# Two blocks on one Trainium2 core: the second block's modulation summed by VectorE, ScalarE and GpSimd instead of TensorE

## The chip, the cores and the metric

The kernel runs on one core of one Trainium2 chip, as one program. The metric is the device time of one execution in microseconds (us), smaller is better. Before the change it was 3041.41 us, the median of three runs (3035.09, 3041.41 and 3043.16).

In the profile PE is TensorE (PEld its weight loads), DVE is VectorE, ACT is ScalarE, POOL is GpSimd and SP is SyncE, which issues nearly all DMAs. L280 is line 280 of the kernel.

## The reference

Two transformer blocks follow each other. The first works on 256 tokens of width 1024, in two layers; the second on the same 256 tokens and 256 context tokens, again in two layers, with a mixer of three branches and 32 experts. The second block is steered by a modulation that depends on two condition vectors alone (the sample's `c` and the context's `c_ctx`), not on the tokens:

```python
def first_block(...):
    h = x
    for i in range(DEPTH):                                  # 2
        g = norm_g[i]
        y = mixer_i(rms_norm(h, g[0]))                      # MLA, then dilated attention
        h = h + rms_norm(y, g[1])
        h = h + rms_norm(swiglu(rms_norm(h, g[2]), ffn_w_in[i], ffn_w_out[i]), g[3])
        h = h + (p[i] @ ple_w_proj[i]) * jax.nn.sigmoid(h @ ple_w_gate[i])
    return h

def ada_modulation(cond, w, b):
    m = cond @ w + b                                        # [1, 1024] @ [1024, 6144]
    return jnp.split(m[:, None, :], 6, axis=-1)

def second_block(x, c, ctx, c_ctx, w_ada, b_ada, ...):
    cond_lat, cond_ctx = jax.nn.silu(c), jax.nn.silu(c_ctx)[None]
    for l in range(DEPTH):                                  # 2
        sh1, sc1, gt1, sh2, sc2, gt2 = ada_modulation(cond_lat, w_ada[l], b_ada[l])
        csh1, csc1, cgt1, csh2, csc2, cgt2 = ada_modulation(cond_ctx, w_ada[l], b_ada[l])
        ...
```

## The kernel before, in words

The program goes through the first block phase by phase: `mla_layer`, `ffn_layer(0)`, `ple_layer(0)`, `dil_layer`, `ffn_layer(1)`, `ple_layer(1)`; then `second()` does the two layers of the second block. All matrix products with weights are float32 products made of three float32r products. A weight tile of 1 MB is loaded from DRAM into one of four `raw` buffers (`load_raw`, NRAW = 4); class `W` splits each half of it into `hi` (ScalarE cast, L279) and `lo` (VectorE subtraction, L280; in the first pair of tiles of a phase it is GpSimd's), each in one of three buffers (NSPLIT = 3); `mm3` issues the three matmuls (L291 to L293).

In `ffn_layer` one pass of the loop (a chunk) computes 256 of 2816 hidden features: two weight tiles, four halves, 96 matmuls of 256 columns; then, per 128 features, silu on ScalarE (L811), a product with the other half in PSUM on VectorE (L812), and the split of the result into `hidh` (ScalarE, L817) and `hidl` (VectorE, L818). There are 11 chunks in each of the two layers. In `dil_layer` each of four quads of heads takes nine such weight tiles of 48 matmuls each, and then its attention.

The modulation is background work: class `Ada` holds a generator per layer of the second block, and `fill(n)` emits n units of it at places of the first block that the table FILL gives. There are 48 units. A unit before loads 1 MB of `w_ada` (128 rows, 2048 columns) into a raw buffer and issues four matmuls (L888), one to each 32 rows of a PSUM bank; eight units accumulate one bank, which is then added to the bias rows `msb` (L892). After three banks, `msb` is transposed (L897), copied to `mod` (L898) and written to DRAM (`dm`, L899). Ten units lie in the attention of `mla_layer`, and by FILL 5 at its end, 10 in quads 2 and 3 of `dil_layer` and 8 at its end, 3 and 3 at the ends of the ffn layers, 3 and 5 at the ends of `ple_layer`; one is left to the start of `second()`.

Instructions stand on each engine in the order in which the tile framework places them, each engine executes its own in that order, and a buffer is given out anew when its readers are done.

Of the kernel before, what the change touches and what calls it, by code (L numbers as in the profile page):

```python
# [7 lines left out]
F32 = mybir.dt.float32  # L8
# [8 lines left out]
D = 1024  # L17
# [21 lines left out]
def build_consts():  # L39
# [36 lines left out]
    # relative bias of the dilated mixer: bucket one-hot over m = t - s + 127  # L76
# [7 lines left out]
    for g, dil in enumerate((1, 4, 16)):  # L84
# [16 lines left out]
def build(nc, tc, I, O, stop=""):  # L101
    """I: dict of input APs, O: output AP [256, 1024]."""
# [47 lines left out]
    def pipelined(n, stages, between=None):  # L150
        """stages[j](i) for items i < n, stage j of an item j steps after its first."""
# [11 lines left out]
    def blk(shape, dt=F32, name="blk", glob=False):  # L163
        """A block of the phase, or one that outlives it."""
# [84 lines left out]
    def load_exp(ap):  # L249
        """4 (or 2) k chunks of an expert's weight, also in buffers of split weights; k -> [128, width]."""  # L250
# [14 lines left out]
    class W:  # L265
        """Rows chunks of a weight tile as pairs (hi, lo)."""
# [29 lines left out]
    def rsqrt(ssq, n, inv_d):  # L296
        """(ssq * inv_d + eps) ** -0.5 for [128, n] sums of squares."""
# [570 lines left out]
    class Ada:  # L868
# [13 lines left out]
        def units(self):  # L882
            for c in range(3):
                p = ps_mm()
                for k in range(8):
# [4 lines left out]
                    if k < 7:  # L890
                        yield
# [869 lines left out]
```

## Time and profile before

| | |
|---|---|
| runs, median | 3041.41 us (3035.09 to 3043.16) |
| the profiled execution, span from its first to its last instruction | 3046.4 us |
| PE busy | 2842.3 us, 93% |
| DVE busy | 1383.3 us, 45% |
| ACT busy | 946.0 us, 31% |
| POOL busy | 384.1 us, 13% |
| HBM read | 697.91 MB, 230 GB/s over the span |
| mean granted TensorE clock | 0.971 |

The page gives no time of the profiled execution beside its span. The first block and the modulation fill about the first 1000 us, the second block the rest. The shares are means over stages with different limits: the busy shares of the stages that the change touches are read from windows of the trace.

### The profile page before, as it was taken

The numbers are of one execution on the slowest core, as the hardware profiler recorded it, in microseconds if no ns is written. First come the engines' busy times: TensorE is split into PE (matmuls) and PEld (weight loads), VectorE is DVE, ScalarE is ACT, GpSimd is POOL, SyncE is SP. The second block draws the span as 40 slices with busy tenths as digits, with TensorE's granted clock in tenths as the row PEclk, the third lists the DMA queues.
The fourth block names the chain that finished last, engine by engine and source line by source line (L and its number), as shares of the span: only waits on it lengthen the run. The fifth ranks groups of instructions, "written<-read, shape, count | busy, mean of one in ns | idle before, by whom it ended". The sixth has DMA issues, their size and how long they took to land. (4 is left out here: it accounts for less than half of the span.)

```text
span 3046.4 us, 39455 instructions
## 1 busy us (share of the span) xinstructions
PE 2842.3 (93%) x15583; PEld 1972.6 (65%) x15583; DVE 1383.3 (45%) x2942; ACT 946.0 (31%) x1630; POOL 384.1 (13%) x304
## 2 busy tenths in 40 slices
PE   7999999998999999999979999999799997999996
PEld 6699789886997786678764444443486894333332
DVE  6555555445555426533472333333537564222222
ACT  5444444333444333433331001010334442111111
POOL 1010000000000201101031322223201001111111
PEclk9999999999999999999989999999899998999999
DMA  6665665665656432113468889889432386999997
GB/s 201 232 204 189 213 207 155 193 201 180 197 184 221 154 93 47 59 49 97 141 228 327 347 347 359 331 346 395 143 125 69 123 278 253 409 398 409 409 409 300
DMA packets 317148, 702.36 MB, mean 231 GB/s; under 512 B 36055, under 2 KB 179694, under 8 KB 310686
## 3 DMA queue, kind: packets, MB, share of 16 engines
q1 hardware_dynamic: 316622, 698.20, 64.0%
q8 instruction: 125, 2.05, 0.3%
q10 hardware_dynamic: 336, 1.59, 0.1%
q14 instruction: 65, 0.53, 0.0%
HBM read 697.91 MB, written 1.81 MB: 230 GB/s over the span
## 5 line engine op out<-in xcount | busy, mean ns | idle before, releaser
L280 DVE TENSOR_TENSOR lo<-raw,hi 128x1024 fp32r<-128x1024 f32 (+1 forms) x404 | 500.7, 1240 | 573.3 <-ACT hi L279 572.4
L279 ACT CAST hi<-raw 128x1024 fp32r<-128x1024 f32 (+1 forms) x418 | 433.7, 1039 | 623.4 <-PE mm L292 341.9
L291 PE MATMUL mm<-xh,hi 128*128 128x256 f32 (+1 forms) x1728 | 544.2, 316 | 3.7 <-ACT hi L279 2.5
L292 PE MATMUL mm<-xl,hi 128*128 128x256 f32 (+1 forms) x1728 | 538.3, 312 | 0.5 <-DVE xl L944 0.5
L293 PE MATMUL mm<-xh,lo 128*128 128x256 f32 (+1 forms) x1728 | 535.2, 310 | 1.2 <-POOL lo L280 1.2
L291 PEld LDWEIGHTS mm<-xh,hi 128*128 128x128 f32 x1728 | 333.4, 193 | 45.1 <-issue 20.3
L1532 PE MATMUL mm<-raw,xq 128*64 128x512 f32 x1152 | 345.3, 608 | 7.1 <-DMA raw<-in_moe_w_up_dram 3.9
L293 PEld LDWEIGHTS mm<-xh,lo 128*128 128x128 f32 x1728 | 333.0, 193 | 18.4 <-issue 1.8
L292 PEld LDWEIGHTS mm<-xl,hi 128*128 128x128 f32 x1728 | 333.5, 193 | 17.5 <-issue 2.0
L1546 POOL TENSOR_TENSOR h<-h,res 128x512 f32<-128x512 f32 x120 | 150.2, 1273 | 758.0 <-DVE res L1544 713.5
L1544 DVE TENSOR_TENSOR res<-tp,gt 128x512 f32<-128x512 f32 x192 | 123.0, 684 | 235.7 <-PE tp L1542 235.7
L1532 PEld LDWEIGHTS mm<-raw,xq 128*64 128x64 f32 x1152 | 100.0, 139 | 175.5 <-issue 156.6
L1601 DVE SCALAR_TENSOR_TENSOR y<-mm,wsum,y 128x512 fp32r<-128x512 f32 x64 | 47.1, 749 | 306.0 <-ACT y L1600 304.0
L291 PE MATMUL mm<-hi,xh 128*128 128x512 f32 (+2 forms) x504 | 174.9, 349 | 0.0
L293 PE MATMUL mm<-hi,xl 128*128 128x512 f32 (+2 forms) x504 | 174.9, 347 | 0.0
L292 PE MATMUL mm<-lo,xh 128*128 128x512 f32 (+2 forms) x504 | 174.4, 346 | 0.0
L1532 PE MATMUL mm<-raw,hT 128*64 128x512 f32 x568 | 160.1, 597 | 12.8 <-ACT hT L1589 12.6
L1532 PE MATMUL mm<-hi,xq 128*64 128x512 f32 x428 | 167.4, 603 | 0.6 <-DMA hi<-in_moe_w_up_dram 0.6
L1532 PE MATMUL mm<-lo,xq 128*64 128x512 f32 x428 | 159.7, 593 | 0.0
L1505 ACT COPY xq<-tp 128x512 f32<-128x512 f32 x64 | 37.5, 587 | 348.6 <-PE tp L1503 348.6
L280 POOL TENSOR_TENSOR lo<-raw,hi 128x1024 fp32r<-128x1024 f32 x14 | 33.7, 2422 | 861.2 <-ACT hi L279 766.0
L1542 PEld LDWEIGHTS tp<-y,oht 128*128 128x128 f32 x384 | 63.7, 188 | 119.3 <-issue 47.9
(486 smaller groups left out, 4588.3 us busy)
## 6 DMA issues: line engine op xcount, KB each, us to landing
raw<-in_moe_w_gate_dram SPq DMA_DIRECT2D x77, 1024.0 KB
raw<-in_moe_w_down_dram SPq DMA_DIRECT2D x71, 1024.0 KB
raw<-in_moe_w_up_dram SPq DMA_DIRECT2D x67, 1024.0 KB
raw<-in_w_in_dram SPq DMA_DIRECT2D x56, 1024.0 KB
raw<-in_w_ada_dram SPq DMA_DIRECT2D x48, 1024.0 KB
raw<-in_ffn_w_in_dram SPq DMA_DIRECT2D x44, 1024.0 KB
raw<-in_dil_w_qkv_dram SPq DMA_DIRECT2D x36, 1024.0 KB
hi<-in_moe_w_up_dram SPq DMA_DIRECT2D x59, 512.0 KB
```

What stands on the lines that cost most here:

```text
L279: A.copy(hv, rv[:, k0:k0 + n, :])
L280: (eng or V).tensor_tensor(lv, rv[:, k0:k0 + n, :], hv.bitcast(F32), op=ALU.subtract)
L291: T.matmul(ps, lhsT=lh, rhs=rh, start=first, stop=False)
L292: T.matmul(ps, lhsT=lh, rhs=rl, start=False, stop=False)
L293: T.matmul(ps, lhsT=ll, rhs=rh, start=False, stop=last)
L1505: A.copy(xq[:, 2 * kk:2 * kk + 2, :], p.rearrange("p (a b) -> p a b", b=256))
L1532: T.matmul(p[n][64 * i:64 * i + 64, :], lhsT=lhs(k, i), rhs=rv[i][kk][:, n * 512:(n + 1) * 512], start=k == 0, stop=k == kn - 1)
L1542: T.matmul(p, lhsT=oht[:, t * 128:(t + 1) * 128], rhs=y[:, i, ns], start=i == 0, stop=i == 1)
L1544: V.tensor_tensor(tmp, p, gts[:, t // 2, ns], op=ALU.mult)
L1546: (G if P < 15 else V).tensor_tensor(hs, hs, tmp, op=ALU.add)
L1601: V.scalar_tensor_tensor(y[:, 1, ns], py[n], wsum, y[:, 0, ns].bitcast(F32), op0=ALU.mult, op1=ALU.subtract)
```

## The change

A unit now loads 1 MB of `w_ada` as two chunks of 128 rows for the 1024 columns of one of the six parameters. VectorE multiplies a row chunk by the sample's condition (one number per partition) and adds it to an SBUF sum (`acc[:, 0]`, one instruction of 1024 columns per row chunk). For the context's condition ScalarE multiplies into a buffer `mtmp` of 512 columns, of which there is one, and GpSimd adds that to `acc[:, 1]`, twice per row chunk. The first row chunk of a parameter writes the sums instead. After four units, four matmuls with a selecting matrix `sel` add up the partitions into a PSUM bank, which is added to `msb`. Four times six units per layer are 48 units, as before, and the same bytes. The units move: none in or after `mla_layer`, one in each chunk of both ffn layers, 22 in `dil_layer`, and 4 at ends of phases. For the memory, a pool `ada` is opened after `mla_layer`, and the temporary tables of the rope move to a small tile. The layout of `msb`, `mod` and `dm` is another.

```diff
-FILL = dict(mla_end=5, ffn=([0] * 11, [0] * 11), ffn_end=(3, 3), ple_end=(3, 5), dil_end=8,
-            dil=([0] * 9, [0] * 9, [1] * 5 + [0] * 4, [1] * 5 + [0] * 4))
+FILL = dict(mla=0, mla_end=0, ffn=([1] * 11, [1] * 11), ffn_end=(1, 1), ple_end=(1, 0), dil_end=1,
+            dil=([1, 0, 1, 0, 1, 0, 1, 0, 1], [1, 0, 1, 0, 1, 0, 1, 0, 1], [1, 0, 1, 1, 0, 1, 1, 0, 1],
+                 [1, 0, 1, 1, 0, 1, 1, 0, 1]))
...
-        condT = cpool.tile([128, 8, 36], F32, name="condT")
-        V.memset(condT, 0.0)
+        condT = cpool.tile([128, 8, 2], F32, name="condT")
+        sel = cpool.tile([128, 40], F32, name="sel")
+        V.memset(sel, 0.0)
+        V.memset(sel[:, 8:9], 1.0)
...
-            for c in range(3):
+            condT = late["condT"]
+            for i in range(6):
+                acc = late["ada"].tile([128, 2, 1024], F32, tag="acc", name="macc")
+                wv = I["w_ada_2"][self.l].rearrange("(a k p) f -> p a k f", k=2, p=128)
+                for kq in range(4):
+                    rv, _, _ = load_raw(wv[:, kq, :, i * 1024:(i + 1) * 1024])
+                    for kk in range(2):
+                        k = 2 * kq + kk
+                        c0, c1 = condT[:, k, 0:1], condT[:, k, 1:2]
+                        if k == 0:
+                            V.tensor_scalar(acc[:, 0], rv[:, kk], c0, None, op0=ALU.mult)
+                            A.activation(acc[:, 1], rv[:, kk], AF.Copy, scale=c1)
+                            continue
+                        V.scalar_tensor_tensor(acc[:, 0], rv[:, kk], c0, acc[:, 0], op0=ALU.mult, op1=ALU.add)
+                        for n in range(2):
+                            tmp = late["ada"].tile([128, 512], F32, tag="mtmp", name="mtmp")
+                            ns = slice(n * 512, n * 512 + 512)
+                            A.activation(tmp, rv[:, kk, ns], AF.Copy, scale=c1)
+                            G.tensor_tensor(acc[:, 1, ns], acc[:, 1, ns], tmp, op=ALU.add)
+                    if kq < 3:
+                        yield
                 p = ps_mm()
-                for k in range(8):
-                    rv, _, _ = load_raw(I["w_ada_2"][self.l, k * 128:(k + 1) * 128, c * 2048:(c + 1) * 2048])
-                    for j in range(4):
-                        T.matmul(p[32 * j:32 * j + 32, :], lhsT=late["condT"][:, k, 4 - 2 * c:36 - 2 * c], rhs=rv[:, j * 512:(j + 1) * 512],
-                                 start=k == 0, stop=k == 7)
-                    if k < 7:
-                        yield
+                for j in range(2):
+                    for cnd in range(2):
+                        r = 32 * (2 * j + cnd)
+                        T.matmul(p[r:r + 32, :], lhsT=late["sel"][:, 8 - i:40 - i], rhs=acc[:, cnd, j * 512:(j + 1) * 512],
+                                 start=True, stop=True)
                 V.tensor_tensor(self.msb, p, self.msb, op=ALU.add)
-                if c < 2:
+                if i < 5:
                     yield
...
     for l in range(2):
-        (dil_layer if l else mla_layer)()
+        if l:
+            dil_layer()
...
+    fill(1000)
+    apool.close()
     second()
```

Ahead of that last loop the change calls `mla_layer()` and opens the pool `ada` with one buffer of each tile. In the `mla_layer` attention it takes the call of `fill` from between the heads.

The order on ScalarE in the middle of `ffn_layer(0)`, one chunk, before (`hi` of the next weight tile, then silu and `hidh` of the chunk that ends):

```order
L279 CAST hi_1858<-raw_1856 128x1024
L279 CAST hi_1862<-raw_1856 128x1024
L811 ACTIVATE silu_1846<-mm_1748 128x256
L817 CAST hidh_1719<-silu_1846 128x256
L279 CAST hi_1868<-raw_1866 128x1024
L811 ACTIVATE silu_1851<-mm_1749 128x256
L817 CAST hidh_1719<-silu_1851 128x256
L279 CAST hi_1872<-raw_1866 128x1024
```

The same on ScalarE after the change (`mtmp` is the buffer that GpSimd adds from, raw_2386 the tile of `w_ada`):

```order
L280 CAST hi_2368<-raw_2366 128x1024
L903 ACTIVATE mtmp_2389<-raw_2386,condT_669 128x512
L280 CAST hi_2372<-raw_2366 128x1024
L903 ACTIVATE mtmp_2392<-raw_2386,condT_669 128x512
L813 ACTIVATE silu_2356<-mm_2258 128x256
L903 ACTIVATE mtmp_2396<-raw_2386,condT_669 128x512
L813 ACTIVATE silu_2361<-mm_2259 128x256
L280 CAST hi_2378<-raw_2376 128x1024
L819 CAST hidh_2213<-silu_2356 128x256
L819 CAST hidh_2213<-silu_2361 128x256
L903 ACTIVATE mtmp_2399<-raw_2386,condT_669 128x512
L280 CAST hi_2382<-raw_2376 128x1024
```

Four operations of the unit now stand between the eight of the chunk, the first of them ahead of the second `hi`, the last behind the second `hidh`.

The order on VectorE in the same chunk after the change (`macc` is the sum `acc`):

```order
L281 TENSOR_TENSOR lo_2369<-raw_2366,hi_2368 128x1024
L899 SCALAR_TENSOR_TENSOR macc_2100<-raw_2386,condT_669,macc_2100 128x1024 x2
L281 TENSOR_TENSOR lo_2373<-raw_2366,hi_2372 128x1024
L814 TENSOR_TENSOR silu_2356<-silu_2356,mm_2258 128x256
L814 TENSOR_TENSOR silu_2361<-silu_2361,mm_2259 128x256
L281 TENSOR_TENSOR lo_2379<-raw_2376,hi_2378 128x1024
L820 TENSOR_TENSOR hidl_2214<-silu_2356,hidh_2213 128x256
L820 TENSOR_TENSOR hidl_2214<-silu_2361,hidh_2213 128x256
L281 TENSOR_TENSOR lo_2383<-raw_2376,hi_2382 128x1024
```

The two multiply-adds stand between the two `lo` of the chunk's first tile; the rest is what the chunk had before.

The order on GpSimd around the start of `dil_layer` after the change (`lo` there are the halves of its first weight tile; before, nothing stood between these and the two `lo` of `ple_layer` ahead of them):

```order
L281 TENSOR_TENSOR lo_3484<-raw_3481,hi_3483 128x1024
L281 TENSOR_TENSOR lo_3488<-raw_3481,hi_3487 128x1024
L904 TENSOR_TENSOR macc_3788<-macc_3788,mtmp_3794 128x512
L904 TENSOR_TENSOR macc_3788<-macc_3788,mtmp_3797 128x512
L904 TENSOR_TENSOR macc_3788<-macc_3788,mtmp_3905 128x512
L904 TENSOR_TENSOR macc_3788<-macc_3788,mtmp_3908 128x512
L904 TENSOR_TENSOR macc_3788<-macc_3788,mtmp_3912 128x512
L281 TENSOR_TENSOR lo_3895<-raw_3892,hi_3894 128x1024
L904 TENSOR_TENSOR macc_3788<-macc_3788,mtmp_3915 128x512
L281 TENSOR_TENSOR lo_3899<-raw_3892,hi_3898 128x1024
```

Five adds of two units now stand ahead of the first of these `lo`, and a sixth between them.

## Rows read from the trace of the kernel before

**Rows 1.** The page, part 1: busy time, share of the span, instructions.

```profile
PE 2842.3 (93%) x15583; PEld 1972.6 (65%) x15583; DVE 1383.3 (45%) x2942; ACT 946.0 (31%) x1630; POOL 384.1 (13%) x304
```

**Rows 2.** Windows: from:to, length, busy PE, PEld, DVE, ACT, POOL, clock, DMA, GB/s.

```profile
70.00:120.00 50.00, 49.16 (x326) 30.46 (x325) 26.34 (x108) 24.50 (x80) 0.00 (x0) 1.00 0.72 260
163.00:295.00 132.00, 132.00 (x1073) 130.62 (x1072) 71.08 (x90) 63.17 (x91) 3.18 (x2) 0.99 0.55 183
400.00:740.00 340.00, 339.19 (x2539) 306.49 (x2539) 164.41 (x385) 134.09 (x216) 0.00 (x0) 1.00 0.60 177
```

**Rows 3.** Windows of line L888 alone (PE, PEld, clock, DMA, GB/s).

```profile
70.00:120.00 50.00, 15.85 (x80) 2.23 (x80) 1.00 0.72 260
400.00:740.00 340.00, 18.99 (x88) 2.65 (x88) 1.00 0.60 177
740.00:760.00 20.00, 8.01 (x56) 1.51 (x56) 0.79 0.86 302
```

**Rows 4.** Timeline of ACT in `ffn_layer(0)`: start, us, instruction, idle before.

```profile
225.65 1.05 ACT L279 CAST hi<-raw 128x1024 fp32r<-128x1024 f32 x1 [1.62 <-issue]
228.54 1.05 ACT L279 CAST hi<-raw 128x1024 fp32r<-128x1024 f32 x1 [1.84 <-PE mm L292]
230.04 0.39 ACT L811 ACTIVATE silu<-mm 128x256 f32<-128x256 f32 x1 [0.46 <-PE mm L293]
...
234.18 0.41 ACT L817 CAST hidh<-silu 128x256 fp32r<-128x256 f32 x1 [1.34 <-DVE silu L812]
...
241.56 0.39 ACT L811 ACTIVATE silu<-mm 128x256 f32<-128x256 f32 x1 [0.46 <-PE mm L293]
```

**Rows 5.** Groups of DVE, 163 to 295 us: busy, mean ns, idle before.

```profile
L280 DVE TENSOR_TENSOR lo<-raw,hi 128x1024 fp32r<-128x1024 f32 x44 | 53.9, 1225 | 50.3 <-ACT hi L279 50.3
L818 DVE TENSOR_TENSOR hidl<-silu,hidh 128x256 fp32r<-128x256 f32 x22 | 9.3, 425 | 9.5 <-ACT hidh L817 9.5
L812 DVE TENSOR_TENSOR silu<-silu,mm 128x256 f32<-128x256 f32 x22 | 9.1, 414 | 0.6 <-ACT silu L811 0.6
```

**Rows 6.** Timelines of POOL and of DVE at 1396 us, in the second block.

```profile
1396.01 1.29 POOL L1219 TENSOR_TENSOR acc<-acc,sg 128x512 f32<-128x512 f32 x1 [1.59 <-DVE sg L1217]
...
1396.03 2.36 DVE L280 TENSOR_TENSOR lo<-raw,hi 128x1024 fp32r<-128x1024 f32 x1
```

**Rows 7.** Groups of the whole span by shape, of POOL, DVE and ACT.

```profile
L1546 POOL TENSOR_TENSOR h<-h,res 128x512 f32<-128x512 f32 x120 | 150.2, 1273 | 758.0 <-DVE res L1544 713.5 <-DVE sid L1510 44.5
...
L1544 DVE TENSOR_TENSOR res<-tp,gt 128x512 f32<-128x512 f32 x192 | 123.0, 684 | 235.7 <-PE tp L1542 235.7
...
L1515 DVE SCALAR_TENSOR_TENSOR o1t<-rows,sid 128x512 f32<-128x512 f32 x32 | 23.9, 748 | 8.3 <-DMA hi<-in_moe_w_up_dram 7.7
...
L1517 DVE TENSOR_SCALAR o1t<-rows,sid 128x512 f32<-128x512 f32 x16 | 7.8, 487 | 0.6
...
L1546 DVE TENSOR_TENSOR h<-h,res 128x512 f32<-128x512 f32 x8 | 5.1, 681 | 0.0
...
L1505 ACT COPY xq<-tp 128x512 f32<-128x512 f32 x64 | 37.5, 587 | 348.6 <-PE tp L1503 348.6
```

**Rows 8.** Timeline of all engines at the start of `dil_layer`.

```profile
384.50 5.13 POOL L280 TENSOR_TENSOR lo<-raw,hi 128x1024 fp32r<-128x1024 f32 x2 [32.19 <-ACT hi L279]
...
384.89 2.54 DVE L857 SCALAR_TENSOR_TENSOR sg<-sg,proj 128x512 f32<-128x512 f32 x1 [1.81 <-ACT sg L856]
...
392.69 0.45 PE L341 MATMUL tp<-consts,xn 128*128 128x128 f32 x1 [6.27 <-DVE xn L371]
```

**Rows 9.** Timelines of SP and PE at the start of `ffn_layer(1)`.

```profile
745.28 19.46 SPq L246 DMA_DIRECT2D raw<-in_ffn_w_in_dram  x5
...
759.64 0.58 PE L291 MATMUL mm<-xh,hi 128*128 128x256 f32 x1 [2.53 <-ACT hi L279]
...
762.08 0.58 PE L293 MATMUL mm<-xh,lo 128*128 128x256 f32 x1 [1.21 <-POOL lo L280]
```

**Rows 10.** Timeline of PE at the start of the second block.

```profile
990.71 1.93 PE L888 MATMUL mm<-raw,condT 128*32 128x512 f32 x8 [2.55 <-DMA raw<-in_w_ada_dram]
```

More of the change, by code (lines that the diff above doesn't have):

```diff
@@ L452, in rope_tables @@
         V.tensor_copy(posf, posi)
-        ang = cpool.tile([128, 2, 16], F32, name="ang")
+        ropes = small(96, name="ropes").rearrange("p (i a b) -> p i a b", a=2, b=16)
+        ang, red, nn = (ropes[:, i] for i in range(3))
         for t in range(2):
             V.tensor_scalar(ang[:, t, :], const("inv"), posf[:, t:t + 1], None, op0=ALU.mult)
-        red = cpool.tile([128, 2, 16], F32, name="red")
-        nn = cpool.tile([128, 2, 16], F32, name="nn")
         V.tensor_scalar(nn, ang, 1.0 / (2 * math.pi), 12582912.0, op0=ALU.mult, op1=ALU.add)
@@ L488, in setup @@
         for cnd in range(2):
-            V.tensor_copy(condT[:, :, 4 + cnd], pt[:, cnd * 8:cnd * 8 + 8])
+            V.tensor_copy(condT[:, :, cnd], pt[:, cnd * 8:cnd * 8 + 8])
         lam_init = [0.8 - 0.6 * math.exp(-0.3 * l) for l in range(2)]
@@ L523, in setup @@
             nbs.append(nb)
-        late.update(condT=condT, neglam=neglam, sublng=sublng, nbs=nbs)
+        late.update(condT=condT, sel=sel, neglam=neglam, sublng=sublng, nbs=nbs)
     def mla_layer():
@@ L679, in mla_layer @@
                 it = iter(range(100))
-                pipelined(8, (scores, probs, turn, values), lambda: fill(next(it) % 2))
+                pipelined(8, (scores, probs, turn, values), lambda: fill(next(it) % 2 * FILL["mla"]))
             late["gbias"] = next(late["gbias"])
@@ L876, in __init__ @@
             V.memset(self.msb, 0.0)
-            for j in range(4):
+            for j in range(2):
                 for cnd in range(2):
-                    r = 32 * j + cnd
-                    SP.dma_start(self.msb[r:r + 5:2], dram(I["b_ada_2"], l * 6144 + j * 512, [[2048, 3], [1, 512]]))
+                    r = 32 * (2 * j + cnd)
+                    SP.dma_start(self.msb[r:r + 6], dram(I["b_ada_2"], l * 6144 + j * 512, [[1024, 6], [1, 512]]))
         def units(self):
-            for c in range(3):
-                p = ps_mm()
-                for k in range(8):
-                    rv, _, _ = load_raw(I["w_ada_2"][self.l, k * 128:(k + 1) * 128, c * 2048:(c + 1) * 2048])
-                    for j in range(4):
-                        T.matmul(p[32 * j:32 * j + 32, :], lhsT=late["condT"][:, k, 4 - 2 * c:36 - 2 * c], rhs=rv[:, j * 512:(j + 1) * 512],
-                                 start=k == 0, stop=k == 7)
-                    if k < 7:
-                        yield
+            condT = late["condT"]
@@ new lines, in units @@
+            for i in range(6):
[18 more added lines that the diff above has]
+                        yield
+                p = ps_mm()
+                for j in range(2):
+                    for cnd in range(2):
+                        r = 32 * (2 * j + cnd)
+                        T.matmul(p[r:r + 32, :], lhsT=late["sel"][:, 8 - i:40 - i], rhs=acc[:, cnd, j * 512:(j + 1) * 512],
+                                 start=True, stop=True)
@@ L897, in units @@
                 T.transpose(pt[:, b * 128:(b + 1) * 128], self.msb[:, b * 128:(b + 1) * 128], ident)
[L898 removed]
+            V.tensor_copy(self.mod, pt.rearrange("p (b g r) -> p b g r", b=4, r=32)[:, :, :, 0:6])
             SP.dma_start(self.dm, self.msb)
@@ L1723, in build @@
         return second()
+    mla_layer()
+    apool = ExitStack()
+    late["ada"] = apool.enter_context(tc.tile_pool(name="ada", bufs=1))
     for l in range(2):
-        (dil_layer if l else mla_layer)()
+        if l:
+            dil_layer()
         if stop == f"mixer{l}":
```

7 lines of the change are left out of this document (2 added, 5 removed).

## The prediction

> **What bounds the kernel now.** I read the shares of the page first, then the busy time by stage, then inside one stage the order of one engine, and last the waits at the seams between stages. The page says that TensorE is busy for 93% of the span, the other engines for 45, 31 and 13% [rows 1]. The windows say where that share is a limit: in the attention of the first layer TensorE is busy for 49.16 of 50 us, in the ffn layer for 132.00 of 132.00, in the dilated layer for 339.19 of 340.00, while VectorE and ScalarE are half busy and GpSimd hardly at all [rows 2]. In these stages a matmul that goes away is time that goes away, as long as the others keep up. The modulation's matmuls take 15.85 us in the first, nothing in the ffn and 18.99 us in the dilated layer (88 records, 11 units) [rows 3]. The rest of its 48 units stand at seams, where TensorE waits for a norm anyway. So the change takes work from the engine that is full; the question is what it puts on the three others in the ffn, where it adds 22 of the 48 units and where there was no matmul to save.
>
> **The price of one operation.** An add of 512 columns takes GpSimd 1.273 us alone [rows 7]. A multiply-add of 1024 columns on VectorE is in no row: one of 512 takes 0.748 us, and from 512 to 1024 columns a two-input operation goes from 0.681 to 1.225 us, 0.544 more [rows 5, 7], so 1.29 us; bounds 1.22 and 1.50 (twice 0.748). The first row chunk's multiply is between 0.49 and 0.97 us (487 ns for 512 columns), say 0.75. ScalarE's multiply is a copy of 512 columns, 0.59 us [rows 7]; four in a chunk are 2.4 us on an engine half idle, at no cost by themselves.
>
> GpSimd and VectorE are not independent. At 1396.01 us an add of 512 columns starts on GpSimd and takes its usual 1.29 us; a `lo` that starts at 1396.03 takes 2.36 us instead of 1.225 [rows 5, 6]. The add kept VectorE out for 1.13 us. At 384.50 GpSimd works at two `lo`, and VectorE's operation of 512 columns takes 2.54 us [rows 8]. VectorE's operations with one input in PSUM do not show it: 684 ns on average beside the adds of the same loop [rows 7]. So I add up VectorE's operations from SBUF and GpSimd's adds as if they were on one engine. The Trainium skill says this too ("SBUF — State Buffer", Who interferes with whom): the two engines share a port pair as an exclusive lock, and an instruction of VectorE with two SBUF inputs is blocked by a GpSimd instruction that reads SBUF, and the other way round, for the whole instruction. By that sentence an add would count 1.273 and not 1.13 us, which makes 0.57 us more per chunk than below and 12 us more in all.
>
> **The ffn, +27 us.** The silu of one chunk starts at 230.04 us, that of the next at 241.56 [rows 4]: a chunk is 11.52 us, all of it TensorE's. VectorE has four `lo` and two `hidl` from SBUF, 4 x 1.225 + 2 x 0.425 = 5.75 us, and 2 x 0.414 from PSUM [rows 5]. A unit adds two multiply-adds, 2.58, and four adds, 4 x 1.13 = 4.52. The sum is 12.85 us, 1.33 more than TensorE needs. One unit in four has a lighter first row chunk: 5.75 + 1.29 + 0.75 + 2.26 = 10.05, below 11.52. But a second loop holds all units. Late in a layer the tile of `w_ada` goes into the buffer that its predecessor had, so its load waits for ScalarE's last multiply of that one. That multiply stands behind `hidh`, which ends at 234.59; the first stands behind a `hi`, at 226.70 at the earliest [rows 4]: 8.5 us from the first to the end of the last (0.59). The load moves 1 MB, 3.5 us at 302 GB/s [rows 3]; with an estimate of 1 us for its issue the next unit starts 13.0 us after the last, 1.5 more than 11.52. Of the waits for TensorE inside, 1.84 and 0.46 us [rows 4], some will shrink, so I take +0.9 for the light unit. The mean is (3 x 1.33 + 0.9) / 4 = 1.22 us, for 22 chunks 27 us. TensorE gets this as a late `hi` or `lo`, because the first multiply and the two multiply-adds stand ahead of the next half's. Bounds: +6 if the buffers cover it all (then only the sums over partitions, 5.5 groups at 1.07, count), +42 with 1.9 us per chunk by the longer lock.
>
> **The attention of the first layer, -11 us.** Ten units of 15.85 us go [rows 3], and nothing comes. TensorE's share was 98%, so up to all of it is gained; but behind a fuller TensorE stands the chain scores, maximum, exponential, transposition through two half-busy engines [rows 2], and matmuls removed from between may leave waits. Bounds -6 and -15.85; I take -11.
>
> **The dilated layer, +1 us.** 18.99 us go [rows 3]; 22 units come, with six groups of four matmuls, 6.4 us at 1.07 (12.6 if split by others). The units stand among the weight tiles. One of these has 48 matmuls, 5.76 us at 11.52 / 96, so nine take 52 us. In quads 2 and 3 six units share them, 8.6 us each: three `lo` (3.68 us) and a unit's mean of 6.4 (three times 7.10, once 4.30) are 10.1, 1.5 too much, 12 times. In quads 0 and 1 it is 10.8 against 10.4, ten times 0.4. Together 21 us; part of it runs on into the quad's attention, where VectorE reads PSUM mostly, so I take two thirds, 14. Sum -19 + 6.4 + 14 = +1; bounds -13 (all covered) and +15.
>
> **The seams, -2 us.** At the start of the dilated layer six adds stand among the two `lo` (5.13 us) of GpSimd, and TensorE waited there 6.27 us for a norm that runs on VectorE [rows 8]: +4 (0 to 8). At the start of the second ffn layer the weights were issued at 745.28, behind seven tiles of `w_ada`, and TensorE waited 2.53 us for `hi` and 1.21 for `lo` [rows 9]; one tile stands there now: -3. At the second block TensorE waited 2.55 us for `w_ada` [rows 10]: -3. At the first ffn layer five units leave a place where TensorE waited for a norm, and one comes: 0 (-4 to +4). All covered makes -6, all against makes +8. The order of SP's loads costs nothing more: 3 MB per chunk of 11.52 us are 273 GB/s, below the 302 of [rows 3]. The few other edits (tables, bias rows, indices) are small loads and short operations beside a busy TensorE: 0.
>
> **The sum.** 27 - 11 + 1 - 2 = +15 us. The profiled execution's 3046.4 us, 5.0 above the median, become 3061; the median 3041.4 becomes 3056, my prediction.
>
> **The rivals.** *The cover holds (28%).* The three pairs of `hi` and `lo` let TensorE run on, and GpSimd's adds fall into VectorE's pauses. Then ffn +6, attention -15.85, dilated layer -13, seams -6: -29, 3013 us. For it: VectorE's pauses before `lo` were 50.3 us in that window [rows 5]. Against it: the sum of 12.85. It decides at 0.80 us per add, (11.52 - 8.33) / 4, against the 1.13 seen. *Nothing to see (17%).* The buffers cover about half of the ffn's excess, +13, and the dilated layer comes out at 0: 13 - 11 + 0 - 2 = 0, 3041 us. The same comes if the attention gains nothing because its matmuls lay beside a wait, and the ffn costs less. *Everything goes at the pace of the shared lock (14%).* An add counts in full, in the dilated layer the delayed `lo` is not made good in the attention, and at the seams the norm's operations stand behind adds: ffn +42, dilated layer +15, attention -6, seams +8: +59, 3100 us. It decides if an add costs VectorE 1.27 us or more, or a unit's chain lasts longer than a chunk. The forecast keeps 41%, with its own range from 3044 to 3081.
>
> **The numbers.** A difference of 0.3%, 9 us, is about what a measurement of this kernel can tell from none. The first rival is faster by more; the second mostly the same; of the forecast's 41% some 8 lie within 9 us; the rest and the last rival are slower. That makes 31% faster, 22% the same, 47% slower. The range goes from 3010, a little under the first rival, to 3095, which leaves out the upper half of the last rival and the edge of the first.
>
> **What would show it.** In the profile after: the period of silu in the ffn at 12.3 to 13 us instead of 11.52, TensorE no longer 132 of 132 there, with waits for `hi` or `lo`; `lo` beside an add at up to 2.4 us, so a mean of `lo` over 1.4; adds on GpSimd at 1.3 to 2.3 us. The attention between 70 and 120 us should end some 11 us sooner. If the silu period stays at 11.5, the first rival is right; if the mean add is short or `lo` stays at 1.23, my price of the lock is wrong; if the dilated layer takes over 350 us, the last rival is.

## The result and the profile after

The changed kernel takes 3139.9 us (3134.3 to 3145.1, four runs) where the kernel before takes 3042.3 (3035.1 to 3046.4): a ratio of 1.0324, 95% interval 1.0306 to 1.0342. It is 98 us slower. The forecast was 3056 us with a range to 3095: the sign was right, the size was wrong, 98 us instead of 15. Its span in the profile is 3135.8 us, 89.4 us over that of before; the profiled execution of before is one of the slower of its kernel, so the profiles lie less far apart than the medians.

Part 1 of the page of the changed kernel answers to [rows 1]:

```profile
PE 2839.1 (91%) x15295; PEld 1984.1 (63%) x15295; DVE 1578.3 (50%) x3045; ACT 1060.8 (34%) x1810; POOL 633.0 (20%) x472
```

TensorE executes 288 matmul records less and is busy for the same time, 3.2 us less than before. That was the first hint: its remaining matmuls must have become slower. The stages, cut in both traces at the first or last matmul of each, tell where the time lies. Windows of before (from:to, length, busy PE, PEld, DVE, ACT, POOL, granted clock, DMA share, GB/s), of the first attention with its output product, the first ffn loop, the dilated layer and the second ffn loop:

```profile
69.58:143.13 73.55, 72.71 (x440) 49.91 (x442) 38.59 (x131) 33.77 (x95) 0.00 (x0) 1.00 0.67 237
...
159.15:288.90 129.75, 129.75 (x1063) 129.64 (x1062) 69.84 (x90) 63.16 (x93) 4.79 (x2) 0.98 0.57 186
...
396.34:741.65 345.31, 344.50 (x2566) 311.25 (x2568) 168.16 (x397) 136.53 (x223) 0.00 (x0) 0.99 0.60 178
...
759.64:889.90 130.26, 129.04 (x1057) 128.75 (x1058) 66.93 (x83) 61.68 (x88) 9.42 (x4) 0.98 0.59 193
```

The same stages of the changed kernel:

```profile
71.42:139.38 67.96, 65.39 (x356) 54.94 (x354) 34.79 (x129) 32.51 (x93) 2.59 (x2) 0.87 0.21 65
...
157.32:314.70 157.38, 142.60 (x1079) 131.85 (x1078) 114.96 (x113) 86.14 (x131) 55.61 (x37) 0.94 0.61 209
...
428.21:803.17 374.96, 347.25 (x2518) 319.88 (x2520) 250.11 (x442) 190.07 (x304) 111.76 (x76) 0.95 0.60 187
...
820.71:982.70 161.99, 145.62 (x1079) 135.07 (x1078) 115.45 (x113) 86.35 (x131) 55.38 (x37) 0.93 0.58 202
```

The two ffn loops are 27.6 and 31.7 us longer, the dilated layer 29.7 us; the first attention is only 5.6 us shorter. Of the stretches between them the one ahead of the dilated layer grows most, by 6.1 us. In each of the three longer stages two things add up: TensorE is idle (14.8, 27.7 and 16.4 us, where it was idle for at most 1.2), and the clock it was granted is lower, 0.93 to 0.95 instead of 0.98 to 0.99, 0.87 instead of 1.00 in the attention. From the first scores to the second block's first product, TensorE's busy time is 901 us against 900, although the modulation's matmuls (63 us in all in the trace of before) are gone from it and only the sums (30 us, at the clock they got) came. Without the records of both, the other matmuls are busy for 872 us against 842; the granted clock over that stretch is 0.93 against 0.97. The lower clock has eaten the difference.

**The lock, in the groups.** VectorE in the first ffn loop after (160 to 315 us; [rows 5] is before), and GpSimd's adds:

```profile
L281 DVE TENSOR_TENSOR lo<-raw,hi 128x1024 fp32r<-128x1024 f32 x42 | 59.4, 1421 | 19.0 <-ACT hi L280 18.4 <-issue 0.5
L899 DVE SCALAR_TENSOR_TENSOR macc<-raw,condT,macc 128x1024 f32<-128x1024 f32 x18 | 31.0, 1723 | 9.1 <-DMA raw<-in_w_ada_dram 8.8
L820 DVE TENSOR_TENSOR hidl<-silu,hidh 128x256 fp32r<-128x256 f32 x21 | 14.5, 703 | 3.3 <-ACT hidh L819 3.3
L814 DVE TENSOR_TENSOR silu<-silu,mm 128x256 f32<-128x256 f32 x21 | 8.4, 413 | 1.8 <-ACT silu L813 1.8
...
L904 POOL TENSOR_TENSOR macc<-macc,mtmp 128x512 f32<-128x512 f32 x36 | 53.3, 1481 | 97.5 <-ACT mtmp L903 97.5
```

`lo` takes 1.42 us instead of 1.23, `hidl` 0.70 instead of 0.43, a multiply-add 1.72 (it is 1.28 where GpSimd is quiet); the product from PSUM stays at 0.41. The excess is 42 x 0.196 + 18 x 0.44 + 21 x 0.278 = 22 us for 36 adds, 0.6 us each.

**The sums, in TensorE's timeline.** The matmuls that add up the partitions, in the same loop:

```profile
257.92 1.92 PE L911 MATMUL mm<-macc,sel 128*32 128x512 f32 x2 [3.29 <-DVE macc L899]
261.26 1.92 PE L911 MATMUL mm<-macc,sel 128*32 128x512 f32 x4 [0.48 <-POOL macc L904]
```

And windows of that stretch, columns as above:

```profile
253.00:259.00 6.00, 2.71 (x16) 1.61 (x14) 4.58 (x3) 2.65 (x4) 2.92 (x2) 0.87 0.51 173
259.00:265.00 6.00, 5.52 (x19) 2.79 (x19) 4.79 (x6) 3.16 (x6) 2.88 (x2) 0.56 0.65 213
265.00:271.00 6.00, 6.00 (x45) 5.03 (x44) 1.82 (x2) 1.69 (x2) 0.00 (x0) 1.00 0.45 161
```

TensorE takes its instructions in order. The sums stand among the matmuls of a chunk; when their turn comes, the last multiply-add on VectorE and the last add on GpSimd are not done, and everything behind waits: 3.29 and 0.48 us here. Then the granted clock is 0.56 for the next six microseconds, close to the lower of its two levels (1.2 of 2.4 GHz): in 259 to 265 us only 19 records pass, against 45 in the six after.

**The reload, in the timelines of ScalarE and SP.** In the same loop, ScalarE's last multiplication of one unit, the first and last of the next, and the first of the one after:

```profile
232.73 0.73 ACT L903 ACTIVATE mtmp<-raw,condT 128x512 f32<-128x512 f32 x1 [1.24 <-POOL macc L904]
...
240.22 0.72 ACT L903 ACTIVATE mtmp<-raw,condT 128x512 f32<-128x512 f32 x1 [3.05 <-DMA raw<-in_w_ada_dram]
...
247.31 0.73 ACT L903 ACTIVATE mtmp<-raw,condT 128x512 f32<-128x512 f32 x1
...
254.44 0.72 ACT L903 ACTIVATE mtmp<-raw,condT 128x512 f32<-128x512 f32 x1 [4.52 <-DMA raw<-in_w_ada_dram]
```

The issues of `w_ada` on SP:

```profile
233.49 0.37 SPq L247 DMA_DIRECT2D raw<-in_w_ada_dram  x1
...
248.06 0.37 SPq L247 DMA_DIRECT2D raw<-in_w_ada_dram  x1
```

The loop of the prediction is there: a load is issued when the last multiplication ends (233.46, then 233.49; 248.04, then 248.06), and the next unit begins when it lands. From issue to first use it took 6.7 and 6.4 us, where I had put 4.5; with 7.8 us from the first multiplication to the end of the last the loop is 14.2 us. The chunk is 157.4 / 11 = 14.3. That the two agree does not show that the reload drives the rest: ScalarE's multiplications wait in it for GpSimd, and stand in one queue with `hi` and silu, which wait for TensorE. Without the sums (e2 below) a chunk with the same loads and multiplications takes 13.3 us.

### The profile page after: what moved, and what is told of

Same layout as the page of the kernel before. It is cut to its first block, busy times and chain, and to the rows that moved or that the text cites. A ratio compares the mean times of both kernels' runs of the same rounds, so it can differ in the third digit from the quotient of the medians.

```text
span 3135.8 us, 39344 instructions
## 1 busy us (share of the span) xinstructions
PE 2839.1 (91%) x15295; PEld 1984.1 (63%) x15295; DVE 1578.3 (50%) x3045; ACT 1060.8 (34%) x1810; POOL 633.0 (20%) x472
## 5 line engine op out<-in xcount | busy, mean ns | idle before, releaser
L281 DVE TENSOR_TENSOR lo<-raw,hi 128x1024 fp32r<-128x1024 f32 (+1 forms) x404 | 539.3, 1338 | 456.2 <-ACT hi L280 453.9
L904 POOL TENSOR_TENSOR macc<-macc,mtmp 128x512 f32<-128x512 f32 x168 | 248.7, 1481 | 597.6 <-ACT mtmp L903 545.1
L903 ACT ACTIVATE mtmp<-raw,condT 128x512 f32<-128x512 f32 x168 | 121.5, 723 | 197.7 <-POOL macc L904 124.9
L899 DVE SCALAR_TENSOR_TENSOR macc<-raw,condT,macc 128x1024 f32<-128x1024 f32 x84 | 140.8, 1676 | 36.2 <-DMA raw<-in_w_ada_dram 35.0
```

Source lines behind the costliest of these rows:

```text
L281: (eng or V).tensor_tensor(lv, rv[:, k0:k0 + n, :], hv.bitcast(F32), op=ALU.subtract)
L899: V.scalar_tensor_tensor(acc[:, 0], rv[:, kk], c0, acc[:, 0], op0=ALU.mult, op1=ALU.add)
L903: A.activation(tmp, rv[:, kk, ns], AF.Copy, scale=c1)
L904: G.tensor_tensor(acc[:, 1, ns], acc[:, 1, ns], tmp, op=ALU.add)
```

## The experiments

Three causes stood open: the shared lock (theory L), the chain and reload between ScalarE, GpSimd and the tile (theory R), and TensorE's waits at the sums with the clock behind them (theories S and C). The experiments take them apart. Those that leave out a part of the modulation change the second block's gates and with them the distribution of tokens to experts; a program path for experts with more tokens than slots may then run, and the whole time says nothing (6410 us for e1, 6482 for e2). Of these I read the stages up to the second block alone, which do not depend on data. The table has the stages of each profile in us, cut as above; the last column is the time of the first product of the second block. Each row is one execution, and e8, e9 and e13 were run only once. The first attention has the same instructions in the changed kernel and in all variants but e4, e12 and e13: twelve rows from 65.2 to 69.7 us, which shows how far a single stage varies without a cause in the code.

| kernel | attention | ffn 0 | dilated | ffn 1 | second block begins |
|---|---|---|---|---|---|
| before | 73.5 | 129.7 | 345.3 | 130.2 | 1002.1 |
| changed | 68.0 | 157.3 | 375.0 | 161.9 | 1095.2 |
| e1_no_context | 66.7 | 130.8 | 334.3 | 131.0 | 986.5 |
| e2_no_sums | 65.2 | 146.5 | 361.2 | 145.2 | 1058.3 |
| e5_late_sums | 66.7 | 153.1 | 376.6 | 154.9 | 1090.4 |
| e6_adds_on_vector | 66.7 | 149.5 | 340.2 | 149.7 | 1034.0 |
| e7_vector_only | 66.7 | 145.6 | 337.8 | 145.7 | 1030.7 |
| e8_no_vector | 69.7 | 150.6 | 369.2 | 152.2 | 1068.9 |
| e9_adds_without_scalar | 67.9 | 170.7 | 391.2 | 168.8 | 1136.8 |
| e10_vector_late_sums | 66.7 | 132.3 | 344.3 | 132.6 | 1002.5 |
| e11_two_buffers | 66.7 | 158.8 | 385.1 | 157.3 | 1112.1 |
| e14_in_place | 66.7 | 162.8 | 366.8 | 162.6 | 1095.6 |
| e15_in_place_vector | 66.7 | 144.9 | 339.8 | 149.9 | 1027.6 |
| e4_attention_units_moved | 64.9 | 128.5 | 355.8 | 131.3 | 1006.5 |
| e13_filler_matmuls | 70.5 | 156.6 | 370.1 | 157.1 | 1088.4 |
| e12_mixed | 73.4 | 131.7 | 338.9 | 131.0 | 998.1 |

### The sums: left out, and later

The first (e2) leaves out the group of selecting matmuls and the addition to `msb`; the second (e5) moves both behind the next `yield`:

```diff
-                    if kq < 3:
-                        yield
+                    yield
                 p = ps_mm()
...
                 V.tensor_tensor(self.msb, p, self.msb, op=ALU.add)
-                if i < 5:
-                    yield
```

> Leaves out the twelve groups of selecting matmuls and their additions to the bias rows, so the modulation is the bias alone; all loads, multiplications and additions into the SBUF sums stay. Theory S (TensorE waits in its own queue for sums that come late, and then works at the lower clock): in the profile of the change 19 us of TensorE's idle time in the ffn and dilated layers end at these matmuls, they take some 16 us themselves, and the clock falls to 0.54 to 0.56 behind them; all three go, the time falls by 35 to 50 us to 3090 to 3105, and each ffn layer from 157 to 162 us to about 140. Theory L (the shared lock and the reload loop set the pace of the weight halves): only the matmuls' own time goes, 3125 to 3135, ffn layers at 150 or more.

> The four matmuls that add up the partitions are issued one unit later (one chunk later in the ffn), all else as in the change. Theory S: the waits at these matmuls and the low clock behind them go, their own time stays: 3095 to 3112. Theory L: the same time as the change, 3135 to 3145, perhaps more, since the first row chunk of the next parameter now waits for the matmuls.

Without the sums the ffn loops took 146.5 and 145.2 us: 11 and 17 less, more than the sums' own time, less than S asked for, and far from 130. The second block begins 36.9 us sooner, which is within S's 35 to 50. But late sums gave 3137.7 us, a ratio to the kernel before of 1.0309 (1.0290 to 1.0328), no gain against the 1.0324 of the change. TensorE's idle time at the sums was gone, and in its place stood 13.7 us (nine times) and 16.0 us (eight times) of waits for `lo` in the two ffn loops. So in the change the sums are where TensorE waits, not why the others are late: S alone is refuted.

### The context's part, and VectorE's part, left out

In e1 the inner loop runs over nothing (`for n in range(0)`), in e8 the multiply-add is deleted, and in e9 ScalarE's multiplication is, so that GpSimd adds the raw tile:

```diff
-                            A.activation(tmp, rv[:, kk, ns], AF.Copy, scale=c1)
-                            G.tensor_tensor(acc[:, 1, ns], acc[:, 1, ns], tmp, op=ALU.add)
+                            G.tensor_tensor(acc[:, 1, ns], acc[:, 1, ns], rv[:, kk, ns], op=ALU.add)
```

> Leaves out ScalarE's multiplications and GpSimd's additions for row chunks 1 to 7 of each parameter, so the context's modulation holds the first row chunk alone; VectorE's multiply-adds, the loads and the matmuls stay. Theory L: without GpSimd's adds VectorE has 9.2 us per chunk of 11.5, the tile is free after the two multiply-adds, and the ffn layers come back to 131 to 137 us, the dilated layer to 350 to 360: 3055 to 3080. Theory S: the sums still wait for VectorE and TensorE for them; 10 to 25 us less than the change, 3115 to 3130.

> Leaves out VectorE's multiply-adds for row chunks 1 to 7 (the sample's modulation holds the first row chunk alone; what follows the first block is another time); ScalarE's multiplications and GpSimd's adds stay as in the change. Theory L: GpSimd's adds and VectorE's lo and hidl are 10.3 us per chunk, below 11.5: ffn layers 129 to 137 us. Theory R: the chain and the tile's return are as before: 145 to 160.

> Leaves out ScalarE's multiplications: GpSimd adds the tile of w_ada itself (the context's modulation is then a plain sum; what follows the first block is another time). As many adds on GpSimd and multiply-adds on VectorE as in the change. Theory L: the sum of both engines is as before, ffn layers 145 to 160. Theory R: four adds in a row give the tile back sooner and ScalarE's queue is free, ffn layers 129 to 140.

e1 is clear: without the context's half both ffn loops are back at 131 us, the dilated layer is 11 us faster than before (334.3 us, below the 350 to 360 that L gave), and the second block begins 15.6 us sooner than before. VectorE's half is thus nearly free; all of the loss comes with the half that ScalarE and GpSimd share. e8 came out as R said, not L: with VectorE's multiply-adds gone there is 10.3 us of locked work per chunk, and the loops still take 151 and 152 us, 9.2 and 8.9 us of it waits for GpSimd's last add at the sums. The chain and the reload, with only `lo` and `hidl` beside them on VectorE, are enough to make the sums late. e9 has as many adds without ScalarE and is the slowest of all, 170.7 and 391.2: beyond L's 145 to 160, and further still from R's 129 to 140. So neither theory holds alone.

### Who adds

e6 changes one letter, GpSimd's add to VectorE's:

```diff
-                            G.tensor_tensor(acc[:, 1, ns], acc[:, 1, ns], tmp, op=ALU.add)
+                            V.tensor_tensor(acc[:, 1, ns], acc[:, 1, ns], tmp, op=ALU.add)
```

e7 does the context's part as VectorE does the sample's; of its edit only the line that replaces the inner loop is shown:

```diff
+                        V.scalar_tensor_tensor(acc[:, 1], rv[:, kk], c1, acc[:, 1], op0=ALU.mult, op1=ALU.add)
```

> The change, but VectorE adds the context's products instead of GpSimd; ScalarE still multiplies into the one buffer of 512 columns. VectorE has 5.75 + 0.83 + 2.58 + 4 x 0.68 = 11.9 us per chunk. If the shared lock is what costs (theory L), the ffn layers take 129 to 138 us each instead of 157 and 162 and the time is 3060 to 3090. If it is the chain from ScalarE's multiply to the add to the next multiply, and the tile that is given back only after the last (theory R), it stays: ffn layers 148 to 162, time 3120 to 3145.

> The change, but VectorE does both multiply-adds, each of 1024 columns; ScalarE and GpSimd have no part in it. VectorE has on average 6.6 + 4.9 = 11.5 us per chunk of 11.5, with no lock and no chain between engines. Theory L and theory R both give ffn layers of 128 to 138 us; if VectorE's own busy time had been the cause, they stay over 145. Time: start of the second block as without the context's part (13 us sooner than before) plus 0 to 20, so 3030 to 3060.

They took 3078.8 us, ratio 1.0128 (1.0108 to 1.0149), and 3083.3 us, 1.0151 (1.0127 to 1.0176). The one letter of e6 is worth 61 us against the change, with ScalarE's multiplications and their one buffer still there. The dilated layer falls from 375 to 340 and 338 us. In the ffn I missed: the 150 us of e6 are what R gave, and the 146 of e7 are what VectorE's own busy time was to give; for the whole time of e7 I had said 3030 to 3060. But all of TensorE's idle time there, 9.0 and 8.5 us in e7, stands before the sums, twice per loop. TensorE in the first ffn loop of e7:

```profile
252.47 3.10 PE L907 MATMUL mm<-macc,sel 128*32 128x512 f32 x8 [5.57 <-DVE macc L899]
```

Four matmuls that take 1.07 us at the full clock wait 5.57 us for VectorE and then take 3.10. So there are two readings of e7, the sums' place and VectorE's busy time; e10 decides.

### The last piece: VectorE alone, with late sums

> Both multiply-adds on VectorE, and the four matmuls that add up the partitions issued one unit later. In the variant without the late sums each ffn layer took 145.7 us, of which 8.5 to 9 us were waits of TensorE at these matmuls and some 6 us the lower clock behind them. Theory S+L (what is left after the lock and the chain are gone is the wait at the sums): ffn layers 129 to 134 us each, time 3083 minus 24 to 30, 3050 to 3062. If VectorE at 11.5 us per chunk is the limit itself: ffn layers 140 and more, time over 3070.

3050.3 us, ratio 1.0028 (1.0016 to 1.0040). The first ffn loop of e7 and then of e10 (columns as above):

```profile
156.10:301.67 145.57, 136.52 (x1079) 130.76 (x1077) 115.40 (x133) 62.78 (x93) 2.40 (x1) 0.96 0.65 218
...
156.15:288.41 132.26, 132.03 (x1078) 129.27 (x1077) 114.67 (x133) 62.41 (x93) 2.40 (x1) 0.99 0.72 245
```

Both ffn loops are at 132 to 133 us, with 0.2 us of idle time in one and none in the other; VectorE is busy for 115 and 113 of them, about as long as in e7. So waiting at the sums and the clock behind it cost e7 some 33 us, 26 of them in the two ffn loops, and VectorE is not yet a limit there. VectorE in e10 from inside the first ffn loop on (175 to 305 us; the loop ends at 288.4), where nothing runs on GpSimd:

```profile
L281 DVE TENSOR_TENSOR lo<-raw,hi 128x1024 fp32r<-128x1024 f32 x45 | 54.9, 1221 | 14.6 <-ACT hi L280 14.6
L899 DVE SCALAR_TENSOR_TENSOR macc<-raw,condT,macc 128x1024 f32<-128x1024 f32 x16 | 20.5, 1279 | 4.4 <-DMA raw<-in_w_ada_dram 4.4
```

1.28 us is what I had estimated for a multiply-add (1.29).

### Lock or queue

In the dilated layer of the change TensorE waits longest for exponentials that come late (five times, 19.7 us in all). ScalarE's timeline there:

```profile
674.62 0.72 ACT L903 ACTIVATE mtmp<-raw,condT 128x512 f32<-128x512 f32 x1 [1.73 <-POOL macc L904]
676.82 0.72 ACT L903 ACTIVATE mtmp<-raw,condT 128x512 f32<-128x512 f32 x1 [1.48 <-POOL macc L904]
677.45 1.03 ACT L280 CAST hi<-raw 128x1024 fp32r<-128x1024 f32 x1
678.92 0.72 ACT L903 ACTIVATE mtmp<-raw,condT 128x512 f32<-128x512 f32 x1 [0.44 <-POOL macc L904]
679.55 0.60 ACT L765 ACTIVATE s<-s,nm 128x384 f32<-128x384 f32 x1
```

And VectorE's and TensorE's at the same place:

```profile
675.59 1.22 DVE L764 TENSOR_SCALAR nm<-nm 128x2 f32<-128x2 f32 x1
```

```profile
680.29 0.90 PE L770 MATMUL tp<-consts,s 128*128 128x128 f32 x3 [6.57 <-ACT s L765]
```

The maximum is ready at 676.81, and the exponential begins at 679.55, behind multiplications that wait for GpSimd to give the one buffer back. That reads as a queue, not as a lock; but the maximum's last operation, a negation of two columns, took 1.22 us beside an add. And another of the five waits in this layer reads the other way, VectorE's negation and then ScalarE's exponential:

```profile
692.80 1.24 DVE L764 TENSOR_SCALAR nm<-nm 128x2 f32<-128x2 f32 x1
```

```profile
694.07 0.61 ACT L765 ACTIVATE s<-s,nm 128x384 f32<-128x384 f32 x1 [1.52 <-DVE nm L764]
```

Here ScalarE is idle and waits for VectorE, which an add from 692.63 to 694.01 held up. Of the 19.7 us of these five waits 11.8 (three) end behind a multiplication that had waited for GpSimd, and 7.9 (two) within 0.1 us of such a negation, in one of them also of a table load on ScalarE. e11 splits the buffer in two of 256 columns; e14 does without the buffer, and e15 is e14 with the adds on VectorE:

```diff
-                            A.activation(tmp, rv[:, kk, ns], AF.Copy, scale=c1)
-                            G.tensor_tensor(acc[:, 1, ns], acc[:, 1, ns], tmp, op=ALU.add)
+                            A.activation(rv[:, kk, ns], rv[:, kk, ns], AF.Copy, scale=c1)
+                            G.tensor_tensor(acc[:, 1, ns], acc[:, 1, ns], rv[:, kk, ns], op=ALU.add)
```

> The change with the context's products in two buffers of 256 columns instead of one of 512 (the same memory, twice as many multiplications and adds of half the width); GpSimd and its lock stay. Theory R (ScalarE's queue stands still while a multiplication waits for GpSimd's add to give the one buffer back, and silu, hi and the exponentials stand behind it): the dilated layer falls from 375 to 345 to 358 us, ffn layers by 5 us or more, time 3090 to 3115. Theory L (the lock by itself): no gain in the dilated layer, 370 to 385, time 3130 to 3155.

> The change, but ScalarE writes the context's products over the tile of w_ada instead of into the one buffer, and GpSimd adds from there: no multiplication waits for an add any more; as many adds on GpSimd as in the change. Theory R (ScalarE's queue stands still behind GpSimd's adds): the dilated layer falls from 375 to 340 to 358 us, time 3080 to 3110. Theory L (GpSimd's adds keep VectorE out, and that alone suffices): the dilated layer stays at 365 to 385, time 3125 to 3150.

> The same, but VectorE does the adds, so GpSimd has no part. Theory L: the dilated layer at 335 to 345, ffn layers at 143 to 150 (the waits at the sums stay), time 3070 to 3090, some 45 to 60 us under the variant with GpSimd. Theory R: within 20 us of the variant with GpSimd.

e11: 3156.6 us, ratio 1.0373 (1.0356 to 1.0389), the dilated layer 385; with twice as many adds it is slower, a little beyond what L gave. e14: 3144.8 us, 1.0345 (1.0324 to 1.0366), as L gave; e15: 3077.1 us, 1.0122 (1.0104 to 1.0140). The pair differs in the engine of the add alone: 68 us, more than the 45 to 60 expected. The dilated layer is 366.8 with GpSimd, 8 less than in the change, and 339.8 without. So without the one buffer 8 us go there, though e14 also gives the tile of `w_ada` back later, after the last add, which works the other way (its first ffn loop is 5.5 us longer than the change's); GpSimd's adds are worth 27. Where VectorE adds, the buffer makes no difference: 340.2 us with it (e6), 339.8 without (e15). VectorE in the dilated layer of e14 (430 to 800 us):

```profile
L281 DVE TENSOR_TENSOR lo<-raw,hi 128x1024 fp32r<-128x1024 f32 x77 | 121.0, 1578 | 24.2 <-ACT hi L280 22.5 <-PE mm L293 1.3
```

The same of e15 (400 to 740 us):

```profile
L281 DVE TENSOR_TENSOR lo<-raw,hi 128x1024 fp32r<-128x1024 f32 x78 | 95.1, 1219 | 19.0 <-ACT hi L280 18.8
L903 DVE TENSOR_TENSOR macc<-macc,raw 128x512 f32<-128x512 f32 x78 | 51.7, 684 | 0.3 <-ACT raw L902 0.2
```

VectorE takes over 52 us of adds, and the stage still ends sooner than with the adds on GpSimd.

### The clock in the attention

e4 is the kernel before with the ten units of the attention moved into quads 0 and 1 of the dilated layer. e13 is the change with groups of four matmuls that nobody reads at the old places:

```diff
+                        pf = ps_mm()
+                        for jf in range(4):
+                            T.matmul(pf[32 * jf:32 * jf + 32, :384], lhsT=late["sel"][:, 0:32], rhs=cm, start=True, stop=True)
```

> The kernel before, with the ten matmul units of the first layer's attention moved into quads 0 and 1 of the dilated layer, where they cost 16 to 21 us as the others do in quads 2 and 3. If the attention gains what these matmuls took (15.9 us), the time stays within 5 us of the kernel before, 3037 to 3047. If TensorE falls to the lower clock without them (theory C: in the profile of the change its granted clock in that stretch is 0.87 instead of 1.00, and the stretch is only 5.6 us shorter), the gain is 4 to 6 us and the time 3050 to 3060.

> The change with groups of four matmuls of 384 columns on a resident tile at the places where the units stood in the first layer's attention; nothing reads them. From the first scores to the end of the output product it was 73.5 us before (granted clock 1.00) and is 68.0 in the change (0.87). Theory C (TensorE kept its clock because of these matmuls): the clock comes back to 0.98 to 1.00 and the stretch takes 66 to 73 us, less than 68 plus the fillers' own 8 to 16 us. If the clock has another cause: it stays below 0.92 and the stretch takes 76 to 84 us.

e4: 3052.4 us, ratio 1.0034 (1.0021 to 1.0048), within the 3050 to 3060 of theory C, but with other terms: the ten units save 8.7 us in the attention, not 4 to 6, and cost 10.5 in the dilated layer, not 16 to 21. The stretch from the first scores to the end of the output product, of e4 and then of e13 (columns as above):

```profile
70.82:135.68 64.86, 62.59 (x360) 52.22 (x362) 34.80 (x129) 30.79 (x92) 0.00 (x0) 0.92 0.25 86
```

```profile
71.08:141.61 70.53, 70.28 (x436) 50.37 (x434) 35.13 (x128) 32.34 (x93) 2.60 (x2) 1.00 0.19 63
```

With the fillers the clock is 1.00 again, and 80 more records, busy for 13.5 us, make the stretch 2.6 us longer than the change's 68.0, and 3.8 longer than the 66.7 us that eight of the twelve equal attentions took. Those twelve have granted clocks of 0.85 (69.7 us) to 0.92 (65.2), most of them 0.90. The matmuls that all these kernels share in the stretch, without the modulation's and the fillers', are busy for 59.0 us before, 59.0 in e13 and 65.4 in the change. So taking matmuls out of that attention gave back a quarter to a half of their 15.85 us (3.9 to 8.3 us); most of the rest is clock that TensorE loses with them. Theory C holds there.

### A version from the pieces

e12 computes the first layer's modulation as before (matmuls, in the attention and at seams) and the second's on VectorE alone with late sums, in the ffn chunks.

> A version that the runs point to: the first layer's modulation by matmuls at the places of the kernel before (ten units in the attention, five behind it, the rest at ends of phases), the second layer's by VectorE alone with late sums, one unit in each ffn chunk and two in the dilated layer, none on ScalarE or GpSimd. The attention keeps its clock (73 to 74 us), the ffn layers cost 0 to 4 us each, the dilated layer loses its ten units of 19 us, the seams before the second ffn layer and the second block lose tiles that stood ahead of weights: 3018 to 3038 against 3042. If VectorE's multiply-adds hold up the ffn layers by over 8 us each, it is no faster, 3040 to 3055.

Over seven runs it took 3050.2 us (3041.6 to 3055.1), ratio 1.0023 (1.0010 to 1.0036): a little slower, and outside the 3018 to 3038 that I gave. The ffn loops cost 2.0 and 0.7 us, as expected, but the dilated layer loses 6.4 us, not 19. In its profile the second block begins at 998.1 us, 4.0 sooner than before, and from there to the end of the span it is 2044.0 us against 2044.3; but this is one of its faster executions (3044.0 us) beside one of the slower ones of the kernel before, so it shows no gain. No complete version here beats the kernel before.

## Why the prediction was wrong

*What bounds, and the direction.* The reading of the profile held: stages where TensorE is full, the ffn as the place where nothing is saved and 22 units come, and the forecast's sign.

*The price of one operation.* The multiply-add was right (1.29 against 1.28); ScalarE's multiplication took 0.72 us, not 0.59. That GpSimd's adds hold up VectorE was right, as the groups and e14 and e15 show (`lo` at 1.58 and 1.22), but a whole add was charged to VectorE, 1.13 us; the groups show 0.6 us of VectorE's time per add in the ffn loop. The Trainium skill ("SBUF — State Buffer", Who interferes with whom) says that an instruction of VectorE with two SBUF inputs contends with one of GpSimd that reads SBUF, and the trace agrees in kind: operations with an input in PSUM stayed at 0.41, those with two in SBUF grew. That error alone made the forecast too high; what was left out was larger.

*The ffn, +27 us.* Measured +59. The step that failed is to take the length of a chunk from the busy time of VectorE and GpSimd added up, 12.85 us: VectorE was busy for 115 of the first loop's 157 us, 10.4 per chunk, and a chunk took 14.3. What filled it were waits of the engines for each other, and three terms were missing or too small. First, "only the sums over partitions, 5.5 groups at 1.07, count" charges the sums with their own time and not with their place, and that only in the lower bound; the +27 has nothing for them. They stand in TensorE's queue and wait for the slowest of three engines; the change loses 8.7 and 9.0 us of idle time there. Second, I left the clock out: behind each such wait the next matmuls ran at about half speed. e7 against e10, 33 us, is the price of both when ScalarE and GpSimd have no part. Third, the chain of multiplication, add and reload was there but undersized: 6.4 to 6.7 us from issue to use, not 4.5 (of which the 1 us for the issue stood on no row), so 14.2 us per unit and not 13.0. Taken out in this order, ScalarE and GpSimd (e7) are 28 of the 59 us and the sums' place (e10) 26, and 5 stay; the other way round the late sums alone (e5) bring 11.

*The attention, -11 us.* Measured -5.6 in the profile of the change, and -3.9 to -8.3 in the traces with the same attention, mostly -6.8: about the small end of my bounds of -6 and -15.85. The step that failed is that removed matmuls give back their time unless the chain is late: the chain was hardly late (2.6 us of idle time against 0.8), but the clock fell to 0.87, and the other matmuls took 6.4 us longer.

*The dilated layer, +1 us.* Measured +29.7, outside its bounds of -13 and +15. "Part of it runs on into the quad's attention" was the wrong step: the attention is where it hurt. The exponentials come late there, because they stand on ScalarE behind multiplications that wait for GpSimd, or because the maximum on VectorE was itself held up by an add; one such wait kept TensorE idle for 6.57 us. These waits were 19.7 of the 27.7 us. The clock, at nothing in the sum, adds to it: the matmuls other than the modulation's are busy for 341 us instead of 328, at 0.95 instead of 0.99. GpSimd's adds are the larger part of the loss (27 us between e14 and e15), the queue at the one buffer the smaller (8 us in e14).

*The seams, -2 us.* The dilated layer's start cost 4.8 us, where +4 was said; the start of the second ffn layer gained 0.5 instead of 3, the second block 2.0 instead of 3, the first ffn layer lost 1.9: about +4 in all. Some 5 us more were lost ahead of the first scores and in the output products and ple layers, which the forecast had at nothing.

*The rivals.* The last rival, everything at the pace of the lock (+59), named the place and the engine, and it was the nearest, with 14%. The measured +98 lies beyond it because it too had no clock and no waits at the sums. The first rival was to be right below 0.80 us per add, and the measured 0.6 is below that; yet it was furthest off, because the sign looked at VectorE's busy time, which was not what set the pace.

What stays open: GpSimd's 68 us hold VectorE's lost time, what follows from it (late sums, lower clock), and a shorter chain, since an add takes 0.68 us on VectorE (e15) and 1.87 on GpSimd (e14); these were not measured apart. Two accumulators in turn, which would take the sums' dependence away without delay, were not tried.

## What to carry to other kernels

Work that leaves a full engine is gained only if nothing in that engine's queue then waits for it: charge the instruction that collects the result with the wait at its place, not with its duration, and issue it well behind its inputs. Busy times added up give no pace where engines hand work to each other: follow one unit through its chain. GpSimd is no free engine beside a busy VectorE: the same adds made this kernel 68 us slower there than on VectorE. And TensorE's matmuls are priced by what the clock does around them: in the attention here, matmuls removed gave back only a quarter to a half of their time.

## What the runs showed of the hardware

The granted clock fell in a stretch where TensorE was idle for only 2.6 of 68 us (0.87; 0.85 to 0.92 in the twelve traces with the same instructions), and 80 small records that nobody reads, busy for 13.5 us, brought it back to 1.00 for 2.6 us of time. In e7, after a wait of 5.57 us at the sums, four matmuls took 3.10 us instead of 1.07; in the change, six microseconds behind such a wait were granted 0.56. VectorE's shortest operations are held up as whole ones are: a TENSOR_SCALAR of two columns, 0.17 us elsewhere, took 1.22 us beside an add on GpSimd. Four of the sixteen in the change took 1.22 to 1.25 us, each while such an add ran.
